# A tile of x that goes into its first product before its root is known

## The chip, the cores and the metric

The kernel runs on one core of a Trainium2 chip. Its metric is the time of one execution on the device in microseconds (us); three runs of the kernel before gave a median of 901.99 us (901.09 to 902.46). A profile comes from one more execution.

## The reference

One layer of an encoder in fp32 on x of 1024 tokens by 1024 channels:

```python
h = rmsnorm(x, norm_g[l])
proj = h @ w_in[l]
q, k, v, za, u, vs, zs, gm = jnp.split(proj, IN_SPLITS, axis=-1)
...
sgo = chunked_spatial_gating(jax.nn.gelu(u, approximate=False),
                             jax.nn.gelu(vs, approximate=False), ...)
...
x = x + y @ w_o[l]
return rmsnorm(x, final_g)

def rmsnorm(x, g):
    y = xf * lax.rsqrt(jnp.mean(xf * xf, axis=-1, keepdims=True) + EPS)
    return (y * g.astype(jnp.float32)).astype(x.dtype)
```

The change touches only the start: the first rmsnorm and the product of h with the columns for vs, which the kernel computes first. The root of a token multiplies its whole row of h, so it may be multiplied on after the product as well: (x * g) @ w times the root gives the same.

## The kernel before

**Products of split numbers.** An fp32 value is cast to fp32r (the high part), and the low part is the difference. A product is the sum of three fp32r matmuls of 128x512: high by high, high by low, low by high. All large products are made as blocks of two by two with seven block products instead of eight, from sums of blocks of h (the forms b11, t1, t2, b21, t3, b22, t4) and sums of blocks of the weights (a11, a12, s1 to s4, a22). `split` makes both parts: the cast on ACT (ScalarE), the difference on DVE (VectorE).

**The first stage.** x comes in eight tiles t of 128 tokens. `scale_of(t)` squares a tile on ACT with a row sum, and `rstd_of` makes the reciprocal root of it with a few small operations on DVE and one Sqrt on ACT. `turned_half` multiplies one half of the tile's channels by the root and by norm_g on DVE and transposes it in four 128x128 matmuls against `ident` into a PSUM bank of the tag sc, which has two banks. `form_of` splits the transposed half into a form. Tiles 0 to 3 (`first_tile`) give b11 and b21, tiles 4 to 7 (`second_tile`) t1 and b22, with raw sums that stay in `xh`. `first_product(t)` multiplies b11 of tile t by a11 (bank mm or tp) and b21 by a12 (bank o); ACT copies the second into `xh`, and `to_x11` adds the first later. Then `by_s1(t)` (t1 by s1, in banks o and sc), `by_s4(t)` (b22 by s4), and further the products of t2, t3 and t4.

**The head.** norm_g is spread over the partitions by matmuls of `ones_r` with its high and low halves (`spread`, into `g_in`); `keep_busy` issues matmuls whose results are not used, four ahead of the spreads and eight behind them.

**Order.** The tile framework orders the instructions of each engine when the program is built, and `after(second, first)` adds an order between two of them without a wait of its own. Each engine then works strictly in its order. The x tiles and weights come over SP's queue. The sums of weights are made by accumulating transfers that GpSimd issues (`add_on`, L606): two onto s1, two onto a11 (which becomes s2), two onto a12 (which becomes s4). ACT and DVE split s1 and s4 with `split_behind` (L651, L652). `feed` keeps the head's matmuls in the order in which they are written.

Lines that matter: L353 the products of later stages, L555 `keep_busy`, L573 `spread`, L619 the square, L629 the scaling, L634 the transposes, L647 and L648 the parts of a form, L674 and L675 the raw sum and the negative copy of `second_tile`, L683 `raw_t2`, L736 the low of the first weights, L750 the products of the first stage, L769 the copy out of bank o.

## Time and profile before

| | |
|---|---|
| median of three runs | 901.99 us |
| the profiled execution | 901.17 us, span 899.4 us |
| busy PE, DVE, ACT, POOL | 889.1, 685.8, 532.0, 149.8 us |
| mean granted TensorE clock | 0.998 |
| first matmul of a product starts | 9.79 us |
| PE idle: 0 to 10, 10 to 20, 880 to 899.4 us | 3.0, 0.5, 6.6 us |

PE is TensorE's matmuls, PEld its weight loads, POOL GpSimd. A row of the order of time has the start from the span's start, the time, engine, line, operation, tiles and count, and in brackets how long the engine was idle before it and what ended that. Times of a group of equal rows overlap at their ends: on ACT and DVE an operation starts about 0.1 us before the one ahead of it has ended, on PE 0.17.

### The profile page before, as it was taken

The page shows a single profiled execution, that of the slowest core. Times are in us where ns is not written, and L with a number is a line of the kernel's source. Part 1 is how long each engine was busy: PE and PEld are TensorE (multiplying, and loading weights), DVE is VectorE, ACT ScalarE, POOL GpSimd, SP SyncE. Part 2 cuts the span into 40 slices and gives each one's busy share as a digit, 9 for nine tenths or more (in the row PEclk, how much of TensorE's full clock was granted, in tenths as well). Part 3 has the DMA queues.
Part 4 walks back from the last instruction along what each step waited for, and adds up shares of the span by engine and source line. Part 5 has one row for each costly group of instructions (what it writes and reads, how often), then busy time and mean ns, then how long its engine had stood idle before and what let it go on. Part 6 is the DMA issues. An engine that isn't in the chain of part 4 may idle for free.

```text
span 899.4 us, 13233 instructions
## 1 busy us (share of the span) xinstructions
PE 889.1 (99%) x4304; PEld 743.7 (83%) x4304; DVE 685.8 (76%) x1251; ACT 532.0 (59%) x1064; POOL 149.8 (17%) x213
## 2 busy tenths in 40 slices
PE   8999999999999999999999999999999999999997
PEld 6788888888888888888888888888888888888885
DVE  7879966666687788888878888646796488479986
ACT  7875533334455567676777776755585376467453
POOL 2322222203030001111210111100121121110012
PEclk9999999999999999999999999999999999999999
DMA  9997888868778767878787788899899789998533
GB/s 327 215 258 218 263 208 175 165 157 260 259 253 284 214 188 213 216 151 214 178 221 227 248 241 194 232 316 365 308 284 376 288 226 259 301 301 282 186 116 118
DMA packets 132750, 213.77 MB, mean 238 GB/s; under 512 B 12777, under 2 KB 61161, under 8 KB 132682
## 3 DMA queue, kind: packets, MB, share of 16 engines
q1 hardware_dynamic: 110072, 149.74, 49.9%
q0 software_dynamic: 22464, 62.93, 31.4%
q8 instruction: 34, 0.56, 0.2%
q14 instruction: 34, 0.28, 0.1%
q10 hardware_dynamic: 146, 0.27, 0.1%
HBM read 147.74 MB, written 86.11 MB: 260 GB/s over the span
## 4 chain that ended last, share of the span: by engine, by line
PE 97%; DMA 1%; ACT 1%; DVE 0%; issue 0%; SPq 0%
PE ps_mm L353 42%; PE ps_o L353 27%; PE ps_tp L353 7%; PE ps_sc L1341 3%; PE ps_sc L353 3%; PE ps_tp L750 2%; PE ps_o L1428 2%; PE ps_tp L1387 2%; PE ps_mm L750 2%; PE ps_o L750 2%; PE ps_tp L1012 2%; PE ps_sc L750 1%; PE ps_sc L634 1%; DMA T_t3h<-in_w_dram 1%; ACT wh L162 0%
## 5 line engine op out<-in xcount | busy, mean ns | idle before, releaser
L162 ACT CAST wh<-s 128x1024 fp32r<-128x1024 f32 (+1 forms) x79 | 79.3, 1006 | 92.8 <-PE ps_mm L353 42.4
L163 DVE TENSOR_TENSOR wl<-wr,wh 128x512 fp32r<-128x512 f32 (+1 forms) x77 | 72.0, 936 | 53.2 <-ACT wh L162 52.6
L163 DVE TENSOR_TENSOR wl<-s,wh 128x1024 fp32r<-128x1024 f32 (+1 forms) x79 | 92.6, 1172 | 11.0 <-ACT wh L162 10.9
L162 ACT CAST wh<-wr 128x512 fp32r<-128x512 f32 (+1 forms) x77 | 63.1, 820 | 59.6 <-PE ps_mm L353 30.5
L353 PE MATMUL ps_o<-T_t1h,wh 128*128 128x512 f32 x148 | 58.6, 396 | 0.0
L353 PE MATMUL ps_o<-T_t1h,wl 128*128 128x512 f32 x148 | 57.7, 390 | 0.0
L353 PE MATMUL ps_o<-T_t1l,wh 128*128 128x512 f32 x148 | 57.6, 389 | 0.0
L1356 ACT ACTIVATE pr<-ps_sc,sm 128x192 f32<-128x192 f32 (+2 forms) x128 | 50.9, 410 | 7.4 <-DVE sm L1350 6.4
L353 PE MATMUL ps_mm<-T_t3h,wh 128*128 128x512 f32 x140 | 54.9, 392 | 0.0
L353 PE MATMUL ps_mm<-T_b11h,wh 128*128 128x512 f32 x140 | 54.9, 392 | 0.0
L353 PE MATMUL ps_mm<-T_b11l,wh 128*128 128x512 f32 x140 | 54.7, 391 | 0.0
L353 PE MATMUL ps_mm<-T_t3h,wl 128*128 128x512 f32 x140 | 54.7, 390 | 0.0
L353 PE MATMUL ps_mm<-T_b11h,wl 128*128 128x512 f32 x140 | 54.7, 390 | 0.0
L353 PE MATMUL ps_mm<-T_t2h,wl 128*128 128x512 f32 x140 | 54.6, 390 | 0.0
L353 PE MATMUL ps_mm<-T_t2h,wh 128*128 128x512 f32 x140 | 54.6, 390 | 0.0
L353 PE MATMUL ps_mm<-T_t2l,wh 128*128 128x512 f32 x140 | 54.5, 390 | 0.0
L353 PE MATMUL ps_mm<-T_t3l,wh 128*128 128x512 f32 x140 | 54.5, 389 | 0.0
L353 PE MATMUL ps_mm<-T_t4h,wh 128*128 128x512 f32 x136 | 53.6, 394 | 0.0
L353 PE MATMUL ps_mm<-T_t4h,wl 128*128 128x512 f32 x136 | 53.2, 391 | 0.0
L353 PE MATMUL ps_mm<-T_t4l,wh 128*128 128x512 f32 x136 | 52.9, 389 | 0.0
L307 POOL DMA_DIRECT2D sums<-in_w_dram x40 | 29.8, 939 | 91.6 <-ACT x L371 42.2
L353 PE MATMUL ps_o<-T_b22h,wh 128*128 128x512 f32 x108 | 42.7, 395 | 0.0
(420 smaller groups left out, 2448.2 us busy)
## 6 DMA issues: line engine op xcount, KB each, us to landing
wr<-in_w_dram SPq DMA_DIRECT2D x86, 256.0 KB
sums<-in_w_dram POOLq DMA_DIRECT2D x20, 512.0 KB, 7.0
s<-sums SPq DMA_DIRECT2D x20, 512.0 KB
q_hl<-qhl SPq DMA_DIRECT2D x16, 512.0 KB
q<-q_hl SPq DMA_DIRECT2D x64, 128.0 KB
y_dr<-x POOLq DMA_DIRECT2D x28, 256.0 KB, 6.7
g<-in_w_dram POOLq DMA_DIRECT2D x12, 512.0 KB, 6.6
wr<-in_w_dram SPq DMA_DIRECT2D x11, 512.0 KB
```

The source lines that it names most:

```text
L162: hi_of.append(nc.scalar.copy(hi, src))
L163: return nc.vector.tensor_sub(lo, src, hi.bitcast(F32))
L307: return lambda: paced(nc.gpsimd.dma_start(dst, src, accum_op=op))
L353: nc.tensor.matmul(acc, lt, rt, start=fresh and k == 0 and n == 0, stop=k == 3 and n == 2, skip_group_check=True,)
L634: turns.append(nc.tensor.transpose(pt[:, i * P : (i + 1) * P], xt[:, k * P : (k + 1) * P], ident[:]))
L750: mm = nc.tensor.matmul(acc[:], lt, rt, start=fresh and k == 0 and n == 0, stop=k == 3 and n == terms[-1], skip_group_check=True,)
L1012: nc.tensor.matmul(pm[:, t * P : (t + 1) * P], xh[:, half * 4 + t, g * P : (g + 1) * P], bias[-1][1][:, g % 4, :], start=True, stop=True,)
L1341: nc.tensor.matmul(sc[:, i, k0:], q_of[:, c, i * P : (i + 1) * P], kt[:, f, k0:], start=f == 0, stop=f == 1,)
L1356: nc.scalar.activation(held_in[c, i], sc[:, i, lo:hi], AF.Exp, bias=nmax[:, c, i : i + 1], scale=-1.0, accum_out=sums[:, c, i : i + 1],)
L1387: nc.tensor.transpose(dst, pr[:, i, block * P : block * P + width], ident[:])
L1428: nc.tensor.matmul(po[:, cs], lt, rt, start=n == 0, stop=n == len(terms) - 1)
```

## The change

Tile 0 no longer waits for its root. DVE multiplies it by norm_g alone (`turn_unscaled`), it is transposed, ACT copies it to `xh`, and eight plain fp32 matmuls (`unscaled_product`) take it as it is against the raw weights a11 and a12, unsplit. ACT multiplies the results in both banks by the root afterwards. For the later products tile 0's forms are made from the copies: `spread_root` lays the root along the columns (a diagonal on ACT, a matmul with ones, two copies on ACT), GpSimd multiplies both copies by it (`scale_unscaled`) and makes the low of b11, ACT and DVE make b21 (`split_unscaled`). The low parts of a form come last in tile 1's product, transposes of tiles 2 to 5 stand behind given matmuls of the products (`amid`), tile 5 is scaled ahead of the second low of s1, and tile 6 ahead of the lows of s4. The head has five matmuls of `keep_busy`, all ahead of the spreads; ones come from one memset, and the halves of norm_g are spread one after the other.

The build's order shows it. On ACT at the head, before, where wr_119 is tile 0, T_t3h and T_t3l the raw weights, ps_sc_196 and ps_sc_204 its turned halves:

```order
L619 ACTIVATE wT_154,st_21_159<-wr_119 128x1024
L137 ACTIVATE st_23_163<-st_21_159,eps_sb 128x1
L734 CAST wh_177<-T_t3h_171 128x512 x2
L162 CAST wh_211<-T_t3h_171 128x1024
L647 CAST T_b11h_150<-ps_sc_196 128x4x128
L619 ACTIVATE wT_154,st_31_183<-wr_175 128x1024
L647 CAST T_b21h_152<-ps_sc_204 128x4x128
```

And now, where ps_sc_168 and ps_sc_175 are the turned halves and st_27_163 is the finished root:

```order
L614 ACTIVATE wT_144,st_23_155<-wr_122 128x1024
L140 ACTIVATE st_25_159<-st_23_155,eps_sb 128x1
L696 ACTIVATE xh_119<-ident,st_27_163 128x128
L677 COPY xh_119<-ps_sc_168 128x512
L784 CAST wh_181<-T_t3h_149 128x512 x2
L677 COPY xh_119<-ps_sc_175 128x512
L165 CAST wh_192<-T_t3h_149 128x1024
```

The first half's copy now stands behind the diagonal, which reads the finished root.

On PE around tile 7, before (ps_o_581 is by_s4(1), wr_230 tile 7, ps_sc_663 by_s1(2)):

```order
L750 MATMUL ps_o_581<-wh_509,T_b22h_400 128x512
L634 MATMUL ps_sc_608<-ident,wr_230 128x128 x4
L750 MATMUL ps_o_581<-wh_509,T_b22h_400 128x512
L750 MATMUL ps_o_581<-wl_510,T_b22h_400 128x512 x2
L634 MATMUL ps_sc_618<-ident,wr_230 128x128 x4
L750 MATMUL ps_o_581<-wh_509,T_b22l_401 128x512 x2
L750 MATMUL ps_o_581<-wh_513,T_b22h_400 128x512 x2
L750 MATMUL ps_o_581<-wl_514,T_b22h_400 128x512 x2
```

And now (ps_o_563 is by_s4(1), wr_223 tile 7, ps_sc_645 by_s1(2)):

```order
L801 MATMUL ps_o_563<-wh_495,T_b22h_378 128x512 x2
L801 MATMUL ps_o_563<-wl_496,T_b22h_378 128x512 x2
L801 MATMUL ps_o_563<-wh_495,T_b22l_379 128x512 x2
L629 MATMUL ps_sc_590<-ident,wr_223 128x128 x4
L629 MATMUL ps_sc_600<-ident,wr_223 128x128 x4
L801 MATMUL ps_sc_645<-T_t2h_360,T_t1h_376 128x512 x2
```

Tile 7's transposes moved from the middle of by_s4(1) to its end, directly ahead of by_s1(2), whose bank has the tag of theirs.

On DVE around tile 6, now (wr_221 is tile 6, wl_492 and wl_496 the lows of s4, wr_223 tile 7); before, the two lows, L652, stood ahead of this scaling, with other rows between them:

```order
L624 SCALAR_TENSOR_TENSOR wr_221<-wr_221,st_107_539,xh_119 128x512 x2
L650 TENSOR_TENSOR wl_492<-T_t3l_150,wh_491 128x1024
L650 TENSOR_TENSOR wl_496<-T_t3l_150,wh_495 128x1024
L723 TENSOR_TENSOR xh_119<-xh_119,ps_sc_544 128x512
L643 TENSOR_TENSOR T_b22l_379<-ps_sc_554,T_b22h_378 128x4x128
L138 TENSOR_SCALAR st_112_579<-st_111_577 128x1
L643 TENSOR_TENSOR T_t1l_377<-xh_119,T_t1h_376 128x4x128
L142 RECIPROCAL st_114_583<-st_113_581 128x1
```

On ACT at the same place, before (st_113_599 is tile 7's root, ps_sc_572 tile 6's second half, ps_sc_618 tile 7's):

```order
L777 ACTIVATE xh_116<-ps_o_581 128x512
L137 ACTIVATE st_113_599<-st_111_595,eps_sb 128x1
L647 CAST T_b22h_400<-ps_sc_572 128x4x128
L675 ACTIVATE x_157<-ps_sc_562 128x512
L647 CAST T_t1h_398<-xh_116 128x4x128
L679 COPY T_t4l_402<-ps_sc_572 128x512
L647 CAST T_b22h_400<-ps_sc_618 128x4x128
L675 ACTIVATE x_158<-ps_sc_608 128x512
```

And now (st_113_581 is tile 7's root, ps_sc_590 and ps_sc_600 its halves):

```order
L642 CAST T_b22h_378<-ps_sc_554 128x4x128
L838 ACTIVATE xh_119<-ps_o_563 128x512
L724 ACTIVATE x_147<-ps_sc_544 128x512
L642 CAST T_t1h_376<-xh_119 128x4x128
L728 COPY T_t4l_380<-ps_sc_554 128x512
L140 ACTIVATE st_113_581<-st_111_577,eps_sb 128x1
L642 CAST T_b22h_378<-ps_sc_600 128x4x128
L724 ACTIVATE x_148<-ps_sc_590 128x512
```

Tile 7's root moved behind the copies and the second cast of tile 6; the cast of its second half ahead of the copy of its first is as it was.

The diff, cut to its core:

```diff
-    plain = mtile([P, D], F32, "wl", 3)[:, 0:HALF]
...
-    nc.vector.memset(plain, 1.0)
+    ones_r = mtile([P, 4, HALF], F32R, "T_b22l", 1)[:, 0, :]
+    g_both = mtile([P, 4, HALF], F32R, "T_t1h", 1)
+    nc.vector.memset(ones_r.bitcast(F32), 1.0)
...
+    for at, engine in ((0, nc.vector), (2, nc.gpsimd)):
+        engine.memset(g_both[:, at : at + 2, :].bitcast(F32), 0.0)
...
-    ones_r = slot("b22l", (P, HALF))
-    ones_made = nc.vector.tensor_copy(ones_r[:], plain)
...
-    keep_busy(4)
-    for n in range(2):
-        for half in range(2):
+    keep_busy(5)
+    for half in range(2):
+        for n in range(2):
             spread(n, half)
-    keep_busy(8)
...
-            after(square, casts[2 * t - 3])
+            after(square, casts[2 * t - 5])
...
-            if len(turns) == 1:
-                feed(turns[0])
+            if t == 1:
+                feed(turns[-1])
...
+    def first_half(t, j, xt, r):
+        name = ("b11", "b21")[j]
+        pt = turned_half(xt, r, j, t)
+        form_of(name, t, by_k(pt[:]))
+        if j:
+            return lambda: nc.scalar.mul(raw_b21(t), pt[:], -1.0)
+        return lambda: nc.scalar.copy(raw_sum(t), pt[:])
...
+    def unscaled(j):
+        return by_k((raw_sum, raw_b21)[j](0))
+    def turn_unscaled(j):
+        xg = x_place(0, 0, j)
+        nc.vector.tensor_mul(xg, x_in[0][:, half_of(j)], g_in[j][:])
+        pt = bank("sc")
+        for k in range(4):
+            feed(nc.tensor.transpose(pt[:, k * P : (k + 1) * P], xg[:, k * P : (k + 1) * P], ident[:]))
+        return nc.scalar.copy((raw_sum, raw_b21)[j](0), pt[:])
+    def unscaled_product(acc, j, *ks):
+        for k in ks:
+            feed(
+                nc.tensor.matmul(
+                    acc[:],
+                    unscaled(j)[:, k, :],
+                    raws[("a11", "a12")[j]][:, k, :],
+                    start=k == 0,
+                    stop=k == 3,
+                    skip_group_check=True,
+                )
+            )
+    def spread_root(r):
+        diagonal, *across = (x_place(1, 1, 0)[:, i * P : (i + 1) * P] for i in range(3))
+        nc.scalar.mul(diagonal, ident[:], r[:])
+        summed = bank("sc")[:, 0:P]
+        feed(nc.tensor.matmul(summed, ones_r[:, 0:P].bitcast(F32), diagonal, start=True, stop=True))
+        nc.scalar.copy(across[0], summed)
+        nc.scalar.mul(across[1], summed, -1.0)
+        return [v.unsqueeze(1).broadcast_to([P, 4, P]) for v in across]
+    def scale_unscaled(j, across):
+        return nc.gpsimd.tensor_mul(unscaled(j), unscaled(j), across[j])
+    def split_unscaled(j):
+        hi, lo = (v[:, :, tokens(0)] for v in hb[("b11", "b21")[j]])
+        raw = unscaled(j)
+        if j:
+            low = split(hi, lo, raw, True)
+            after(hi_of[-1], casts[5])
+            after(low, lows[5])
+            return
+        after(nc.scalar.copy(hi, raw), casts[3])
+        return nc.gpsimd.tensor_tensor(lo, raw, hi.bitcast(F32), op=ALU.subtract)
     def second_tile(t):
         xt, r = scale_of(t)
...
+                after(firsts[-1], turned[0])
                 first_lows.append(
                     (nc.gpsimd if k else nc.vector).tensor_tensor(
                         lo[:, ks], raw[:, k, :], hi[:, ks].bitcast(F32), op=ALU.subtract
...
         return mm
     accs = {}
+    steps = []
     t5s = {}
+    def amid(t, half, product, n):
+        turn, step = turns[8 * (t - 1) + 4 * half], steps[24 * (product - 1) + n]
+        after(turn, step)
     def first_product(t):
         accs[t] = bank("mm" if t < 2 else "tp")
-        terms = (0, 1, 2) if t else (0, 2, 1)
-        vs_product(accs[t], "b11", t, "a11", True, terms=terms)
         m2 = bank("o")
-        vs_product(m2, "b21", t, "a12", True, terms=terms)
+        for acc, name, weight in ((accs[t], "b11", "a11"), (m2, "b21", "a12")):
+            if t == 1:
+                vs_product(acc, name, t, weight, True, terms=(0, 1))
+                vs_product(acc, name, t, weight, False, terms=(2,))
+            else:
+                vs_product(acc, name, t, weight, True)
         nc.scalar.copy(x_place(0, 0, t), m2[:])
     def to_x11(t):
...
     def keep_t5(t):
         nc.scalar.copy(x_place(0, 1, t), t5s[t][:])
-    first = scale_of(0)
     for name, at in (("a11", "t3h"), ("a12", "t3l")):
         raws[name] = slot(at, dt=F32)
     load_vs(0)
     load_vs(1)
     x_in[1] = load_x(1)
-    first_lows = []
+    first_lows, firsts = [], []
+    _, root = scale_of(0)
+    turned = [turn_unscaled(j) for j in range(2)]
+    after(turned[0], of_root[0])
...
+    unscaled_product(accs[0], 0, 0, 1)
+    unscaled_product(accs[0], 0, 2, 3)
+    split_vs(1)
+    after(hi_of[0], turned[1])
     second = scale_of(1)
-    unsplit = first_tile(0, first)
-    after(of_mean[1], lows[0])
-    after(first_lows[0], scalings[1])
-    after(lows[0], first_lows[0])
-    split_vs(1)
-    after(first_lows[2], lows[0])
-    after(lows[1], first_lows[2])
-    after(casts[0], hi_of[0])
-    after(squares[1], casts[0])
-    after(casts[1], squares[1])
+    after(squares[1], hi_of[0])
+    after(of_mean[1], first_lows[2])
     for c in (2, 3):
         load_vs(c)
     x_in[2] = load_x(2)
...
-    for c in (2, 3):
-        split_vs(c)
-        after(first_lows[c + 1], lows[1])
-        after(hi_of[c - 1], casts[1])
-    for move in unsplit:
+    m2 = bank("o")
+    split_vs(2)
+    after(hi_of[1], of_root[1])
+    unscaled_product(m2, 1, 0, 1)
+    across = spread_root(root)
+    unscaled_product(m2, 1, 2)
+    split_vs(3)
+    left = [first_half(1, 0, *second)]
+    unscaled_product(m2, 1, 3)
+    left.append(first_half(1, 1, *second))
+    after(hi_of[2], hi_of[1])
+    after(first_lows[3], scalings[1])
+    after(first_lows[4], first_lows[3])
+    after(lows[0], first_lows[4])
+    copied = left.pop(0)()
+    m2_kept = nc.scalar.mul(x_place(0, 0, 0), m2[:], root[:])
+    after(m2_kept, copied)
+    for move in left:
...
-    for c in range(2):
-        add_on(flat(two_k(raws["s1"], c)), w_vs(1, 1, c))
-    for c in range(2):
-        add_on(flat(two_k(raws["a11"], c)), flat(two_k(raws["s1"], c)))
-    for c in range(2):
-        add_on(flat(two_k(raws["a12"], c)), flat(two_k(raws["a11"], c)))
+    sums_begun = [add_on(flat(two_k(raws["s1"], c)), w_vs(1, 1, c)) for c in range(2)]
+    sums_begun += [add_on(flat(two_k(raws["a11"], c)), flat(two_k(raws["s1"], c))) for c in range(2)]
+    sums_begun += [add_on(flat(two_k(raws["a12"], c)), flat(two_k(raws["a11"], c))) for c in range(2)]
...
-    first_tile(1, second)
-    after(scalings[2], first_lows[4])
+    first_tile(2)
+    after(of_mean[2], lows[0])
+    after(lows[1], scalings[3])
+    after(squares[2], casts[0])
+    after(casts[1], of_root[2])
+    after(m2_kept, casts[1])
+    after(nc.scalar.mul(accs[0][:], accs[0][:], root[:]), casts[3])
...
-    first_tile(2)
-    first_product(0)
...
+    after(of_mean[3], lows[1])
+    after(lows[3], scalings[4])
...
+    amid(2, 0, 1, 13)
+    amid(2, 1, 1, 18)
+    for j in range(2):
+        after(scale_unscaled(j, across), sums_begun[1])
+    after(sums_begun[2], split_unscaled(0))
+    after(sums_begun[3], sums_begun[2])
+    after(sums_begun[4], sums_begun[3])
...
-        split_behind(hi, lo, two_k(raws["s1"], c))
+        low_of_s1 = split_behind(hi, lo, two_k(raws["s1"], c))
...
-    second_tile(4)
+        if c == 0:
+            second_tile(4)
...
+    amid(3, 0, 2, 7)
+    amid(3, 1, 2, 13)
+    split_unscaled(1)
...
-    for c in range(2):
-        split_w("s4", c, behind=True)
+    amid(4, 0, 3, 3)
+    amid(4, 1, 3, 9)
+    amid(5, 0, 3, 17)
+    amid(5, 1, 3, 21)
+    after(low_of_s1, scalings[9])
+    lows_of_s4 = [split_w("s4", c, behind=True) for c in range(2)]
...
+    after(lows_of_s4[0], scalings[11])
+    after(highs_behind[2], of_root[6])
```

More of the change, by code (lines that the diff above doesn't have):

```diff
@@ L554, in keep_busy @@
         for _ in range(n):
-            feed(nc.tensor.matmul(idle[:], ones_r[:, 0:P], ones_r[:], start=True, stop=True))
+            feed(nc.tensor.matmul(idle[:], ones_r[:, 0:P], ones_r, start=True, stop=True))
     idle = bank("sc")
     g_in = [bank("tp") for half in range(2)]
-    g_both = slot("t1h")
     g_parts = [g_both[:, 2 * n : 2 * n + 2, :] for n in range(2)]
-    for half in range(2):
-        after(nc.vector.memset(g_parts[0][:, half, :].bitcast(F32), 0.0), ones_made)
-    nc.gpsimd.memset(g_parts[1].bitcast(F32), 0.0)
     for half in range(2):
@@ L574, in spread @@
         )
-    keep_busy(4)
-    for n in range(2):
-        for half in range(2):
+    keep_busy(5)
+    for half in range(2):
+        for n in range(2):
             spread(n, half)
-    keep_busy(8)
     hb = new_b(("b11", "b21"))
@@ L648, in form_of @@
             lows.append(nc.vector.tensor_sub(lo, src, hi.bitcast(F32)))
+    highs_behind = []
     def split_behind(hi, lo, src):
[L651 to L666 removed]
+        highs_behind.append(nc.scalar.copy(hi, src))
+        after(highs_behind[-1], casts[-1])
+        low = nc.vector.tensor_sub(lo, src, hi.bitcast(F32))
+        after(low, lows[-1])
+        return low
@@ L717, in split_w @@
         hi, lo = pair_of_w()
-        (split_behind if behind else split)(hi[:], lo[:], flat(two_k(raws[name], c)) if src is None else src)
+        low = (split_behind if behind else split)(hi[:], lo[:], flat(two_k(raws[name], c)) if src is None else src)
         keep_w(name, c, hi, lo)
+        return low
     def split_vs(c):
@@ L733, in split_vs @@
                 ks = half_of(k)
[L734 removed]
+                firsts.append(nc.scalar.copy(hi[:, ks], raw[:, k, :]))
+                after(firsts[-1], turned[0])
                 first_lows.append(
```

25 lines of the change are left out of this document (8 added, 17 removed).

## The prediction

> **What bounds the kernel now.** I read the page's first part, then the stretches of time, then the first 52 us of PE, ACT and DVE in order of time.
>
> ```profile
> span 899.4 us, 13233 instructions
> PE 889.1 (99%) x4304; PEld 743.7 (83%) x4304; DVE 685.8 (76%) x1251; ACT 532.0 (59%) x1064; POOL 149.8 (17%) x213
> ```
>
> TensorE is busy in 889.1 of 899.4 us, so an edit pays only by ending PE's idle time or its work. The stretches say where the idle 10.3 us are (columns: stretch, length, then busy time and count of PE, PEld, DVE, ACT, POOL, then granted clock, DMA share, GB/s).
>
> ```profile
> 0.00:10.00 10.00, 7.00 (x25) 4.90 (x26) 6.70 (x15) 7.00 (x12) 2.99 (x9) 1.00 0.80 284
> 10.00:20.00 10.00, 9.46 (x43) 7.02 (x43) 8.97 (x20) 8.89 (x17) 1.92 (x2) 1.00 1.03 388
> 40.00:50.00 10.00, 9.92 (x51) 7.72 (x50) 9.31 (x22) 6.30 (x14) 4.04 (x5) 1.00 1.00 243
> 60.00:80.00 20.00, 20.00 (x90) 16.56 (x89) 15.69 (x24) 16.37 (x22) 4.25 (x6) 1.00 0.79 237
> 160.00:880.00 720.00, 720.00 (x3498) 605.22 (x3497) 545.61 (x987) 433.18 (x901) 102.93 (x148) 1.00 0.82 242
> 880.00:899.40 19.40, 12.78 (x68) 10.89 (x66) 12.63 (x36) 6.45 (x18) 5.05 (x6) 0.93 0.28 108
> ```
>
> 3.0 us lie in the first ten, 0.5 in the second, 6.6 in the last 19.4. From 60 to 80 and from 160 to 880 PE is busy without a break, so what the change delays or gains before 60 us arrives at the end one for one. And from 40 to 50 DVE is busy 9.31 of 10 us: there PE runs only just ahead of it.
>
> **Up to the first product.** The head on PE, then ACT and DVE (start, length, instruction, idle time before and what ended it):
>
> ```profile
> 2.19 2.08 PE L555 MATMUL ps_sc<-T_b22l 128*128 128x512 f32 x4 [2.19 <-DVE T_b22l L544]
> 4.07 1.81 PE L573 MATMUL ps_tp<-T_t1h,T_b22l 128*128 128x512 f32 x4
> 5.71 2.02 PE L555 MATMUL ps_sc<-T_b22l 128*128 128x512 f32 x8
> 9.79 0.73 PE L750 MATMUL ps_mm<-wh,T_b11h 128*128 128x512 f32 x2 [0.71 <-ACT T_b11h L647]
> ...
> 4.50 1.06 ACT L619 ACTIVATE wT<-wr 128x1024 f32<-128x1024 f32 x1 [0.27 <-DMA wr<-in_x_dram]
> 5.68 0.29 ACT L137 ACTIVATE st<-st,eps_sb 128x1 f32<-128x1 f32 x1
> 13.24 0.59 ACT L663 COPY xh<-ps_sc 128x512 f32<-128x512 f32 x1
> ...
> 3.81 1.28 DVE L568 TENSOR_TENSOR T_t1h<-wh,T_t1h 1x512 fp32r<-1x512 f32 x2 [0.59 <-ACT T_t1h L567]
> 6.01 0.16 DVE L139 RECIPROCAL st<-st 128x1 f32<-128x1 f32 x1 [0.17 <-ACT st L137]
> 6.91 1.41 DVE L629 SCALAR_TENSOR_TENSOR wr<-wr,st,ps_tp 128x512 f32<-128x512 f32 x2
> ```
>
> Before, the first useful product starts at 9.79; the 12 fillers of L555 are no useful work. Now: the cast L544, which ended PE's first wait, goes, so fillers start about a 512-column DVE operation (0.7) before 2.19, near 1.5, five of them ahead of the four spreads. The spreads still wait for the halves of norm_g (L568, 3.81 to 5.09); both of the first half come first now, so g_in[0] is there near 5.1 and g_in[1] near 5.9. The new multiplications by norm_g cost half of L629's row each, 0.66 start to start: they end near 5.9 and 6.8. Between and behind them stand the small operations of the root. From the reciprocal at 6.01 to the scaling at 6.91 they took 0.9; behind the second multiplication that ends near 7.6 (6.81 before). On ACT the diagonal (L696) needs the finished root and stands ahead of the copy of the turned half 0, as the order in the part on the change shows. ACT thus idles from 5.97 to 7.65 with that copy queued behind, though its transposes are done by 6.6. The diagonal, 128x128, lies between the 0.29 of the one-column root and the 0.59 of a 512-column copy, nearer the first: 0.3. The copy takes 0.59. The first plain product can start at 7.65 + 0.3 + 0.59 = 8.5: 1.3 earlier.
>
> **The plain products.** Matmul pairs in steady state, the wait before tile 1, its transposes, and a group of four transposes later on:
>
> ```profile
> 12.94 0.62 PE L750 MATMUL ps_o<-wh,T_b21h 128*128 128x512 f32 x2
> 13.39 0.62 PE L750 MATMUL ps_o<-wh,T_b21l 128*128 128x512 f32 x2
> ...
> 16.23 1.17 PE L634 MATMUL ps_sc<-ident,wr 128*128 128x128 f32 x8 [0.41 <-DVE wr L629]
> 17.53 0.73 PE L750 MATMUL ps_mm<-wh,T_b11h 128*128 128x512 f32 x2
> ...
> 20.43 0.63 PE L634 MATMUL ps_sc<-ident,wr 128*128 128x128 f32 x4
> 20.81 0.48 PE L750 MATMUL ps_o<-wh,T_b21h 128*128 128x512 f32 x1
> ```
>
> A fp32r matmul of 512 columns costs 0.455 / 2 = 0.227. From 9.79 to 17.53 (7.74) PE did tile 0's 24 (5.45), spent 1.3 on transposes (16.23 to 17.53) and waited the remaining 1.0, 0.41 of it for tile 1's scaling. The 24 become eight plain fp32 matmuls, of which the trace has none. Lower end: one such row, 0.227 each, 1.8 in all. Upper end: a full product of two numbers split in high and low is four products; the kernel spends three, so 4 x 0.227 = 0.91 each and 7.3 in all. I take the upper end: the kernel's own three products leave one out and are the nearest row to a full-width result. With 0.25 for the root's spread, and 1.1 for eight transposes (8 x 0.11 and the refill), tile 1's product starts at 8.5 + 7.3 + 0.25 + 1.1 = 17.15, 0.4 earlier. At the lower end tile 1's own chain sets it (square, root, scalings and transposes, behind the same ACT casts): near 15.4, 2.1 earlier.
>
> The Trainium skill, "FP8 and Floating Point Precision", section "TensorE Precision Notes", gives true FP32 four passes through the array; by it the sum would be the upper end's. No run shown so far bears on it.
>
> **Tiles 1 to 5.** The matmuls are the same in number. From tile 1's product to tile 5's first transposes PE has 66 matmuls (15.0) and six groups of four transposes; a group moves the next matmul by 0.38 plus some 0.1 (row 20.43 to 20.81), 2.8 in all. So the half-0 transposes of tile 5 stand at 17.15 + 17.8 = 35.0, against 36.03 before for both halves. This is the last place with a gain.
>
> **Tiles 6 and 7.** The rows of before:
>
> ```profile
> 36.03 1.18 PE L634 MATMUL ps_sc<-ident,wr 128*128 128x128 f32 x8
> 41.74 1.23 DVE L652 TENSOR_TENSOR wl<-T_t3l,wh 128x1024 fp32r<-128x1024 f32 x1 [0.30 <-ACT wh L651]
> 42.88 0.16 DVE L139 RECIPROCAL st<-st 128x1 f32<-128x1 f32 x1
> 43.72 1.42 DVE L629 SCALAR_TENSOR_TENSOR wr<-wr,st,xh 128x512 f32<-128x512 f32 x2
> 45.23 0.69 DVE L674 TENSOR_TENSOR xh<-xh,ps_sc 128x512 f32<-128x512 f32 x1
> 45.84 0.16 DVE L139 RECIPROCAL st<-st 128x1 f32<-128x1 f32 x1
> 47.17 0.74 DVE L629 SCALAR_TENSOR_TENSOR wr<-wr,st,xh 128x512 f32<-128x512 f32 x1
> ...
> 44.57 0.29 ACT L137 ACTIVATE st<-st,eps_sb 128x1 f32<-128x1 f32 x1
> 46.42 0.61 ACT L675 ACTIVATE x<-ps_sc 128x512 f32<-128x512 f32 x1
> 49.98 0.59 ACT L647 CAST T_b22h<-ps_sc 128x512 fp32r<-128x512 f32 x1 [1.96 <-PE ps_sc L634]
> 50.47 0.60 ACT L675 ACTIVATE x<-ps_sc 128x512 f32<-128x512 f32 x1
> 51.62 0.61 PE L750 MATMUL ps_sc<-T_t2h,T_t1h 128*128 128x512 f32 x2
> ```
>
> Before, tile 7's two groups of transposes lay inside by_s4(1), and by_s1(2) followed at 51.62 without a wait; its bank had come free when ACT's L675 (50.47 + 0.60) had read tile 7's first half. Now all matmuls of by_s4 stand ahead of tile 7's transposes and by_s1(2) directly behind them (order of PE in the part on the change). It needs that same bank, and on ACT the cast of the second half stands ahead of the copy of the first. From the last transpose PE must therefore wait for its end (0.2), the cast (49.98 to 50.47: 0.49) and the copy (0.60), about 1.3. Nothing covers it: PE has no other instruction in between.
>
> When do these transposes come? By DVE's order: from 35.7 the sub of tile 5 (0.60, as 45.23 to 45.84), scaling of its second half (0.66), low of s1 (1.23 by row 41.74, 1.14 start to start), two form lows (1.2), two sums of raw_t2 with a short wait for ACT (1.6), to 40.8; small operations to the scaling (42.88 to 43.72: 0.84), tile 6's scaling (1.33), both weight lows (2.3), sub of tile 6 (0.60): 45.9. ACT then does three copies at 0.49 and only then tile 7's root (0.3), 47.7; before, that root came at 44.57, ahead of them. From the reciprocal to the scaling 1.33 (45.84 to 47.17): 49.1, against 47.17. First half scaled at 49.9, second at 50.6; transposes 50.0 and 50.7 to 51.1, with PE waiting 0.5 and 0.2; with the wait of 1.3 by_s1(2) starts at 52.4 to 52.6. That is 0.8 to 1.0 later than 51.62.
>
> SP's queue keeps its rows and order; the loads of x that wait until tiles 0 to 2 are turned are read several tiles later. Tile 0's forms cost PE nothing: GpSimd's multiplications and its low lie behind the two sums onto s1, and DVE loses one low.
>
> ```profile
> 7.26 1.28 POOL L736 TENSOR_TENSOR wl<-T_t3h,wh 128x512 fp32r<-128x512 f32 x1 [4.97 <-ACT wh L734]
> 24.60 0.86 POOL L606 DMA_DIRECT2D T_t3h<-T_t4h  x1 [7.58 <-DVE T_t1l L629]
> 35.03 0.85 POOL L606 DMA_DIRECT2D T_t3l<-T_t3h  x1 [1.70 <-DVE st L150]
> 40.63 1.08 ACT L651 CAST wh<-T_t3l 128x1024 fp32r<-128x1024 f32 x1
> ```
>
> Three operations of 1.28 (row 7.26) end near 26.2, behind ACT's cast near 24.9; the third sum, issued at 24.60 before, is then issued 1.6 later. The sixth, issued at 35.03, was read by the cast at 40.63; that cast moves to 41.2. Cover 0.5 plus whatever it had landed early; gone, each us late is a us at by_s4. Taken as nothing.
>
> **Sum.** At the first product -1.3; PE's own work after it 8.65 instead of 7.74, +0.9; so -0.4 at tile 1. Then the start of by_s1(2) by its chain, 52.5 against 51.62: +0.9. The same by PE's waits: -0.4, plus 2.0 at tile 7 (0.5, 0.2, 1.3), less the 0.08 that PE idled there from 40 to 50 before: +1.5, if no small wait on the way goes. I take +1.0, nearer the chain, which follows single rows. It is carried to the end. The profiled execution took 901.17 (span 899.4), so 902.2; the median of the three runs is 0.82 above it, 901.99, so 903.0.
>
> **The rivals.** (1) Slower: the clock. Fillers and spreads ran 0.427 apart from 2.19 to 5.35, and 0.23 from 5.71 on (2.08 and 2.02 for 4 and 8): half speed and full, though the granted clock's column shows 1.00 for the whole stretch, so the spacing is the witness. PE had then been busy 3.5 us without a break. The eight fillers behind the spreads are gone; from 5.9 to 8.5 PE has eight transposes and idles half the time. Granted by 5, as busy from 1.5 suggests, nothing happens. If it isn't granted by 8.5, a plain product costs 4 x 0.427 = 1.71, 0.8 more each; one or two are hit before the clock comes: 903.8 to 904.6. It decides once the grant comes after 8.5. The Trainium skill, "TensorE: Matmul & The Clock Gate", Parts 1 and 4, says the activity window is free-running and transposes do not count as busy; that rule speaks against this change. This trace, with full speed 3.5 us after the first matmul, cannot tell a free-running window from one that starts with the work. (2) The GpSimd sums land late: by_s4 waits 0.5 to 1.5 more: 903.5 to 904.5. For it: the third is issued 1.6 later; against: the casts that read the last two come later too. (3) Plain products are cheap: PE is at tile 1 by 15.4, but the waits at tile 7 stay since orders are fixed and DVE is full: about -0.1, 901.9. (4) Faster: cheap products and a DVE that keeps pace, so that 2.1 comes through less the 1.3 or less: 899.9 to 901.2. Little speaks for it: DVE's 9.31 of 10 us.
>
> **How the numbers follow.** Forecast 0.50 (903.0, own range 902.0 to 903.8); clock 0.22; late sums 0.12; cheap products 0.10; faster 0.06. About 0.2%, 1.8 us, is what a measurement of this kernel tells from no change: 900.2 to 903.8. The clock's case is slower but for its lowest end (0.20), late sums in half (0.06), the forecast's upper edge with unknown waits 0.10: slower 0.36. Faster: 0.05 of the last case. Same: 0.59. The range 901.2 to 905.0 leaves out the faster case and, above, two hits of the clock together with late sums.
>
> **What would show it.** Right: the first plain product near 8.5 behind ACT's copy, 0.9 per plain product, tile 1's product near 17.1, an idle time of 1.3 on PE ahead of by_s1(2) at 52.5, ended by ACT's copy of tile 7. Wrong: rows at half clock behind 8.5; by_s4 waiting for a weight low; no idle time at 52.

## The result

The changed kernel takes 904.96 us (median of 16 runs, 902.05 to 907.26) against 901.31 us of the kernel before (16 runs, 900.62 to 902.46). The ratio is 1.0039, 95% interval 1.0029 to 1.0049: slower by some 3.5 us, twice what a measurement of this kernel can tell from no change. It lies inside the range that was given (901.2 to 905.0), but at its upper edge. The likeliest forecast, 903.0 and no change that can be measured, was wrong: "slower" had the smaller chance, 0.36. The runs also spread over 5.2 us, those of before over 1.8.

The profiled execution took 902.81 us and is one of the quickest of the 16. Its page, and its stretches (columns as before):

```profile
span 901.0 us, 13209 instructions
PE 889.2 (99%) x4291; PEld 741.2 (82%) x4291; DVE 684.8 (76%) x1248; ACT 532.6 (59%) x1068; POOL 153.2 (17%) x216
```

```profile
0.00:10.00 10.00, 7.18 (x21) 4.05 (x22) 5.32 (x12) 6.59 (x13) 2.15 (x9) 1.00 0.80 300
10.00:20.00 10.00, 9.87 (x37) 5.73 (x35) 8.78 (x18) 9.00 (x17) 5.31 (x5) 1.00 1.03 373
40.00:50.00 10.00, 9.68 (x48) 7.70 (x47) 9.25 (x20) 6.29 (x12) 5.89 (x7) 1.00 1.00 262
160.00:880.00 720.00, 719.48 (x3493) 604.29 (x3493) 544.45 (x985) 431.27 (x897) 102.65 (x148) 1.00 0.82 242
```

PE's idle time up to 20 us fell (7.18 and 9.87 busy against 7.00 and 9.46). From 40 to 50 it grew (9.68 against 9.92), and from 160 to 880, where PE had not paused at all, 0.5 us is idle. The rows of PE at the places of the prediction:

```profile
1.45 2.50 PE L555 MATMUL ps_sc<-T_b22l 128*128 128x512 f32 x5 [1.45 <-DVE T_b22l L103]
8.41 3.70 PE L683 MATMUL ps_mm<-T_t3h,xh 128*128 128x512 f32 x8 [1.02 <-ACT xh L677]
11.95 1.88 PE L683 MATMUL ps_o<-T_t3l,xh 128*128 128x512 f32 x4
16.40 0.71 PE L801 MATMUL ps_mm<-wh,T_b11h 128*128 128x512 f32 x2
20.21 0.63 PE L629 MATMUL ps_sc<-ident,wr 128*128 128x128 f32 x4 [0.35 <-DVE wr L624]
34.87 0.60 PE L629 MATMUL ps_sc<-ident,wr 128*128 128x128 f32 x4
49.72 1.18 PE L629 MATMUL ps_sc<-ident,wr 128*128 128x128 f32 x8 [0.32 <-DVE wr L624]
52.08 0.74 PE L801 MATMUL ps_sc<-T_t2h,T_t1h 128*128 128x512 f32 x2 [1.18 <-ACT x L724]
...
758.39 0.50 PE L356 MATMUL ps_mm<-T_t4h,wh 128*128 128x512 f32 x1 [0.40 <-DVE x L429]
```

The first plain product starts at 8.41, tile 1's product at 16.40 (17.53 before), tile 5's half-0 transposes at 34.87 (36.03 before). At tile 7 the gain is gone: PE waits 0.32 for DVE's scaling and 1.18 for ACT's copy, and by_s1(2) starts at 52.08 (51.62 before). Two things are not in the prediction: the wait of 0.35 ahead of tile 2's transposes, and the wait at 758.39. In this trace by_s1(2) is 0.46 late and the end 1.6. So the trace shows less than half of the 3.5 us. The rest had to be looked for in other executions of the same kernel.

### The profile page after: what moved, and what is told of

It is laid out like the page before. It is cut to its first block, busy times and chain, and to the rows that moved or that the text cites. A ratio compares the mean times of both kernels' runs of the same rounds, so it can differ in the third digit from the quotient of the medians.

```text
span 901.0 us, 13209 instructions
## 1 busy us (share of the span) xinstructions
PE 889.2 (99%) x4291; PEld 741.2 (82%) x4291; DVE 684.8 (76%) x1248; ACT 532.6 (59%) x1068; POOL 153.2 (17%) x216
## 4 chain that ended last, share of the span: by engine, by line
PE 95%; DVE 3%; ACT 1%; issue 0%; DVEq 0%; ACTq 0%
PE ps_mm L356 42%; PE ps_o L356 27%; PE ps_tp L356 6%; PE ps_sc L1434 3%; PE ps_sc L356 3%; PE ps_tp L801 2%; PE ps_o L1521 2%; PE ps_tp L1480 2%; PE ps_mm L801 2%; PE ps_tp L1105 2%; PE ps_sc L801 1%; PE ps_o L801 1%; PE ps_sc L629 0%; DVE wr L624 0%; PE ps_sc L555 0%
## 5 line engine op out<-in xcount | busy, mean ns | idle before, releaser
L166 DVE TENSOR_TENSOR wl<-wr,wh 128x512 fp32r<-128x512 f32 (+1 forms) x77 | 71.9, 935 | 52.8 <-ACT wh L165 52.1
L166 DVE TENSOR_TENSOR wl<-s,wh 128x1024 fp32r<-128x1024 f32 (+1 forms) x79 | 92.2, 1167 | 11.5 <-ACT wh L165 11.3
```

Source lines behind the costliest of these rows:

```text
L166: return nc.vector.tensor_sub(lo, src, hi.bitcast(F32))
```

## The experiments

The theories at the start: the wait at tile 7 makes the loss (the prediction's step); the software sums land late (its second rival); the clock (its first rival). A fourth came out of the first traces: GpSimd's multiplications stop DVE. A fifth came out of the traces of the repaired kernels: the change shifts the places where PE's code is fetched. Medians of the kernels that were timed, each against runs of the kernel before on the same chip:

| kernel | median us | ratio to before | 95% interval |
|---|---|---|---|
| changed kernel | 904.96 | 1.0039 | 1.0029 to 1.0049 |
| sums_first | 905.27 | 1.0046 | 1.0033 to 1.0059 |
| clock_kept | 904.45 | 1.0034 | 1.0021 to 1.0046 |
| late_forms | 902.59 | 1.0014 | 1.0005 to 1.0023 |
| root7 | 902.29 | 1.0009 | 1.0000 to 1.0018 |
| two | 901.01 | 0.9995 | 0.9985 to 1.0004 |
| three | 900.52 | 0.9991 | 0.9982 to 1.0000 |
| pad10 | 900.21 | 0.9987 | 0.9979 to 0.9996 |
| pad20 | 901.96 | 1.0009 | 1.0000 to 1.0017 |
| best | 899.72 | 0.9981 | 0.9972 to 0.9990 |

**The changed kernel again.** No edit; two more executions with a trace.

> The changed kernel itself, unaltered, one more execution with its trace; the runs of it lie between 902 and 907, and the first trace was of one of the quickest (span 901.0). If the time is lost where the prediction put it (tile 7), this trace too has idle times of about 0.3 and 1.2 ahead of tile 7's transposes and of by_s1(2), and whatever it takes beyond 902.8 lies elsewhere. If the software sums land late, the sixth sum (landed at 40.1 in the first trace) lands later by as much as the run is longer, the casts of s4 (39.9) and the scaling of tile 6 (41.3) follow it, and PE waits ahead of by_s4 or at tile 7. If the clock is late, the first plain products are 1.7 apart instead of 0.86.

> As the look before: a third execution of the changed kernel. Tile 7's wait: idle times of 0.3 and 1.2 at 49.7 and 52.1. Late sums: the sixth sum lands behind 40.1 and by_s4 or tile 7 waits longer. Late clock: plain products 1.7 apart behind 8.4. If the time beyond 902.8 lies in none of these, PE's idle time after 60 shows it.

They took 904.63 and 903.76. Tile 7's two waits are the same in both (0.34 and 1.18), but by_s1(2) starts at 53.08 and 53.09, a whole us later than in the first trace: something ahead of tile 7 varies. In look1 it is the clock. PE's first product, then stretches of look1:

```profile
8.26 5.40 PE L683 MATMUL ps_mm<-T_t3h,xh 128*128 128x512 f32 x8 [1.02 <-ACT xh L677]
```

```profile
6.00:8.00 2.00, 1.08 (x8) 0.60 (x6) 1.13 (x5) 0.74 (x3) 0.00 (x0) 1.00 1.02 410
9.00:10.00 1.00, 1.00 (x2) 0.34 (x1) 0.45 (x1) 1.00 (x3) 0.68 (x1) 0.50 1.05 430
10.00:11.00 1.00, 1.00 (x3) 0.39 (x2) 0.29 (x1) 1.00 (x2) 0.59 (x1) 0.50 1.02 418
```

The granted clock (third column from the end) is 0.50 at 9 to 11, and the four plain products of the first bank took 5.40 instead of 3.70. The trace's clock records put full speed from 4.91 to 8.32, half from 8.32 to 11.73, full from then on: the clock had been granted and was taken back, after a window in which PE idled almost half the time. In look2 the clock stayed and another row is long. DVE's root of tile 2, GpSimd's multiplications, and PE's wait:

```profile
17.76 2.03 DVE L145 SCALAR_TENSOR_TENSOR st<-st,st 128x1 f32<-128x1 f32 x1
```

```profile
16.92 2.85 POOL L704 TENSOR_TENSOR xh<-xh 128x512 f32<-128x512 f32 x2
```

```profile
21.22 0.63 PE L629 MATMUL ps_sc<-ident,wr 128*128 128x128 f32 x4 [1.17 <-DVE wr L624]
```

An operation on one column that takes 0.22 elsewhere took 2.03. It ends at 19.79, GpSimd's second multiplication at 19.77. In the first trace it was the next such operation, less long:

```profile
18.13 1.04 DVE L153 TENSOR_TENSOR st<-st,st 128x1 f32<-128x1 f32 x1
```

```profile
16.24 2.92 POOL L704 TENSOR_TENSOR xh<-xh 128x512 f32<-128x512 f32 x2
```

It ends at 19.17, GpSimd's work at 19.16. This is where PE's 0.35 ahead of tile 2 comes from. A row shortly ahead of it was stopped too, by the first multiplication alone, which by the trace ended at 17.90:

```profile
17.57 0.34 DVE L145 SCALAR_TENSOR_TENSOR st<-st,st 128x1 f32<-128x1 f32 x1
```

**Tile 7's root and scaling early** (root7):

```diff
-    highs_behind = []
+    highs_behind, negated = [], []
...
-        nc.scalar.mul(nf12[t - 4][:], pt[:], -1.0)
+        negated.append(nc.scalar.mul(nf12[t - 4][:], pt[:], -1.0))
...
     after(second_tile(7), move)
+    after(negated[2], of_root[7])
+    after(lows[10], scalings[12])
+    after(lows[11], scalings[12])
```

> The changed kernel with one thing more: ACT takes tile 7's root ahead of the negated copy of tile 6's first half, and DVE scales tile 7's first half ahead of tile 6's two form lows. If tile 7's wait is the loss, PE has no idle time at 49 to 52 any more (0.32 and 1.18 go), by_s1(2) starts near 50.3, and the median falls by 1.5 to 1.9 from the changed kernel's, to about 903.2. If the sums landing late (or anything else that varies) makes the loss, the median falls by less than 0.7 and the spread of the runs stays at 5.

Measured 902.29: 2.7 below the changed kernel, more than the 1.5 to 1.9 expected. Tile 7's transposes lie inside by_s4(1) again and by_s1(2) follows without a wait (51.93, not the 50.3 expected), although this trace had the longest stop of DVE of all:

```profile
15.29 4.26 DVE L166 TENSOR_TENSOR s<-T_t3l,s 128x1024 fp32r<-128x1024 f32 x1
```

```profile
15.64 2.83 POOL L704 TENSOR_TENSOR xh<-xh 128x512 f32<-128x512 f32 x2
```

```profile
20.21 1.19 PE L801 MATMUL ps_mm<-wh,T_b11l 128*128 128x512 f32 x4 [1.97 <-DVE st L138]
```

DVE's low of 1024 columns, 1.22 elsewhere, took 4.26: GpSimd's work ends at 18.47, and 1.08 later, most of its own time, so does the low. The wait at tile 7 is thus a true part of the loss, but not all of it.

**The third sum early** (sums_first), by orders on GpSimd alone:

```diff
-        after(scale_unscaled(j, across), sums_begun[1])
-    after(sums_begun[2], split_unscaled(0))
+        scaled = scale_unscaled(j, across)
+        after(scaled, sums_begun[1])
+        after(sums_begun[2], scaled)
     after(sums_begun[3], sums_begun[2])
-    after(sums_begun[4], sums_begun[3])
+    low_of_b11 = split_unscaled(0)
+    after(low_of_b11, sums_begun[3])
+    for later in sums_begun[4:]:
+        after(later, low_of_b11)
```

> The changed kernel with GpSimd's low of tile 0 (1.29) issued behind the third and fourth software sums instead of ahead of them, so that the third is issued when the first has landed (near 23.6 instead of 26.2). If late sums make the loss: the third sum lands near 30, the sixth near 38 instead of 40.1, the median falls by 1 to 3 and the spread of the runs from 5 to about 2. If tile 7's wait is the loss: the time stays within 0.3 of the changed kernel's, since DVE's order holds tile 6's scaling at 41.3 whatever the sums do.

Measured 905.27, the changed kernel within the error. GpSimd's issues of the third and fifth sum, here and then in the changed kernel:

```profile
24.30 0.87 POOL L601 DMA_DIRECT2D T_t3h<-T_t4h  x1 [4.92 <-DVE st L153]
...
32.58 0.86 POOL L601 DMA_DIRECT2D T_t3l<-T_t3h  x1 [2.66 <-DMA T_t3h<-T_t4h]
```

```profile
26.20 0.87 POOL L601 DMA_DIRECT2D T_t3h<-T_t4h  x1
...
32.78 0.85 POOL L601 DMA_DIRECT2D T_t3l<-T_t3h  x1 [4.10 <-DVE st L138]
```

The third sum was issued 1.9 earlier, but the fifth, which needs it landed, only 0.2 earlier: an earlier issue hardly moved the landings. So this kernel alone does not decide. ACT's casts that read the last two sums do, here in the changed kernel's first trace:

```profile
39.90 1.99 ACT L648 CAST wh<-T_t3l 128x1024 fp32r<-128x1024 f32 x2
```

They start without a wait in every trace. The sixth sum landed at 40.13 in this one (39.92 before the change) and was read by the second cast at 40.84. Late sums are not the loss, and this rival falls.

**More fillers** (clock_kept):

```diff
         for n in range(2):
             spread(n, half)
+    keep_busy(3)
```

> The changed kernel with three more fillers behind the spreads of norm_g (some 0.7 of work ahead of the transposes of x times norm_g, in time in which PE idles, since the copy on ACT is not due before 7.65). In two of the four traces so far of kernels with the change's head (look1, sums_first) the granted clock went back to 0.50 from 8.3 to 11.7, and eight records of plain products took 5.40 instead of 3.70. Clock theory: with the fillers no trace shows 0.50 between 5 and 890, the eight records take 3.70, and the median falls by 0.5 to 1.0 (about half of the executions times 1.0 to 1.7), with no change at tile 7. Port theory: waits for DVE of 0.35 to 2 near 20 remain, and where the clock stays the times are those of look2 and of the first trace, 902.8 to 904: the median falls by less than 0.5.

Measured 904.45. Its trace kept the clock (3.70 for the eight records) and had DVE's stop (2.35 instead of 0.22, PE waits 1.50). The step from 1.0039 to 1.0034 lies inside the intervals, so what the clock costs the median is not shown.

**GpSimd's multiplications later** (late_forms). All orders stay; GpSimd alone waits until DVE has scaled tile 2:

```diff
-        after(scale_unscaled(j, across), sums_begun[1])
+        scaled = scale_unscaled(j, across)
+        after(scaled, sums_begun[1])
+        behind(scaled, scalings[3])
```

> The changed kernel, its orders unchanged, but GpSimd's two multiplications of tile 0's forms wait until DVE has scaled tile 2 (scalings[3]), so that they run from about 19.8 to 22.7 instead of 16 to 19.5. Port theory: DVE operations with two operands in SBUF stood still until GpSimd's two multiplications had ended (1.04 instead of 0.16, 2.03 instead of 0.22, in root7 4.26 instead of 1.22); here none of DVE's operations from 14 to 20 is longer than usual, PE's idle time ahead of tile 2's transposes (0.35, 1.17, in root7 1.97) goes, and the median falls by 0.5 to 1.5. Clock theory alone: no change of the median beyond 0.3, and 5.40 in part of the traces. If GpSimd has nothing to do with it, DVE's long operations come back at another place.

Measured 902.59, 2.4 below the changed kernel, more than the 0.5 to 1.5 expected. The same DVE rows as above, and GpSimd's:

```profile
15.36 1.22 DVE L166 TENSOR_TENSOR s<-T_t3l,s 128x1024 fp32r<-128x1024 f32 x1
...
17.41 0.22 DVE L145 SCALAR_TENSOR_TENSOR st<-st,st 128x1 f32<-128x1 f32 x1
...
17.86 0.16 DVE L153 TENSOR_TENSOR st<-st,st 128x1 f32<-128x1 f32 x1
...
21.67 0.49 DVE L145 SCALAR_TENSOR_TENSOR st<-st,st 128x1 f32<-128x1 f32 x1
```

```profile
19.61 2.53 POOL L704 TENSOR_TENSOR xh<-xh 128x512 f32<-128x512 f32 x2 [3.66 <-DVE wr L624]
```

All three have their usual length. What moved is the next root, tile 3's, stretched from 0.22 to 0.49 until GpSimd ended at 22.14, where DVE has time to spare. One wait on GpSimd, which is no bottleneck, brought back two thirds of the loss: the stops of DVE by GpSimd are shown. Tile 7's waits are still there in this trace (0.33 and 1.18), so this gain is not root7's.

**Both, and with the fillers** (two = root7 and late_forms; three = two and clock_kept).

> Three without its three fillers: tile 7 early and GpSimd's multiplications behind tile 2's scaling. If the clock takes a share, part of the executions run the first plain products at half speed, the spread is wider than three's (899.7 to 902.1) and the median lies 0.3 to 0.8 above 900.5. If the fillers do nothing, the median is 900.5 within 0.2. Port and tile 7 theory: 4.0 to 4.5 below the changed kernel's 904.96.

> All three repairs on the changed kernel: tile 7's root and scaling early (as root7), GpSimd's multiplications behind tile 2's scaling (as late_forms), three fillers (as clock_kept). If these three causes are the whole loss, tile 1's product starts near 16.3, by_s1(2) near 50.2 without a wait (51.6 before), and the median is 1 to 1.5 below that of the kernel before, some 4.5 below the changed kernel's. If something behind 60 us loses more (the traces of the changed kernel lose another 0.8 to 1.9 from 230 to 760), it lies 0.2 to 0.5 below before or level with it.

Two measured 901.01, three 900.52. Alone the two repairs bring 2.7 and 2.4, together 4.0: they overlap. That what DVE loses at 18 us is handed down DVE's order to tile 7's scaling is the likely reason and was not tested. The 0.5 of the fillers lies inside the intervals again. Three's trace is 2.09 ahead of before's at 54 us, yet only 0.55 at the end. Something behind 60 us gives the gain back.

**The kernel before again.** No edit.

> The kernel before, unaltered, a second execution with its trace. All traces of the changed kernel fall behind the first trace of before by 0.2 to 1.3 at 230 to 320 and by 0.4 to 0.7 at 757. If this belongs to the change, this trace lies within 0.2 of the first one from 60 on; if it varies from execution to execution, it shows steps of its own at these places.

It took 901.50. It runs 0.22 behind the first trace of before at 54 us (its clock was granted at 8.24, not 5.62, and its first product starts at 10.04, not 9.79) and 0.32 at the end, with one step of 0.32 near 320 and none at 757. So the step at 757 belongs to the change.

**PE's code at its old places** (pad10, pad20: ten or twenty small matmuls on top of three, behind its three fillers; best: ten, still smaller, where PE waits for ACT's first copy).

```diff
     keep_busy(3)
+    for _ in range(10):
+        feed(nc.tensor.matmul(idle[:, 0:64], ones_r[:, 0:P], ones_r[:, 0:64], start=True, stop=True))
```

> The kernel of three with ten small matmuls more (128x64 into the fillers' bank, behind the three fillers, in PE's idle time), so that PE's stream of instructions has as many matmuls and weight loads as before the change and its code is fetched at the same instructions as before. Three's trace was 2.09 ahead of before at 54 us and only 0.55 ahead at the end: 1.2 lost from 303 to 312, 0.67 at 757, where a software sum that ACT casts at 740 landed 9.2 after its issue (8.0 in both traces of before) and a 16 KB fetch of code ran within it (at 730.1 to 731.9, issue 730.6; before: 730.1 to 731.1, issue 731.8). Code theory: the sum takes 8.0 again, the step at 757 goes, and the median falls by 0.5 to 1.2, to about 899.6. Transfer theory (the transfers themselves are the bound at these places, so that PE cannot keep a lead of over some 1 us): steps of the same size stay and the median stays at 900.5.

> As pad10 with twenty small matmuls: ten more than before the change. PE's code is then fetched about 1 us of PE's work earlier than before. Code theory: it matters where the fetches fall, and the steps at 303 to 312 and 757 change in size (gone or larger), with the sum at 740 between 8.0 and 9.2. Transfer theory: the steps are those of three. Either way some 0.3 is lost at the first product, since the transposes come later.

The wait at 757 goes back to ACT, which waits at 740 for a software sum (bq). By that ACT is late for a low on DVE, and DVE, which does not pause again, is late to read out the bank that PE takes at 757. These are DVE's rows now, and its reading of that bank before:

```profile
743.96 1.23 DVE L166 TENSOR_TENSOR wl<-s,wh 128x1024 fp32r<-128x1024 f32 x1 [0.68 <-ACT wh L165]
...
757.66 0.67 DVE L429 TENSOR_TENSOR x<-x,ps_mm 128x512 f32<-128x512 f32 x1
```

```profile
756.01 0.68 DVE L426 TENSOR_TENSOR x<-x,ps_mm 128x512 f32<-128x512 f32 x1
```

GpSimd's issue of this sum, then ACT's cast, before the change, with the transfers between the two (queue, packets, MB, share):

```profile
731.84 0.86 POOL L205 DMA_DIRECT2D bq<-bq  x1 [1.10 <-DVE wl L163]
```

```profile
739.88 1.06 ACT L157 ACTIVATE T_t2h<-bq 128x1024 fp32r<-128x1024 f32 x1 [0.46 <-DMA bq<-bq]
```

```profile
q0 software_dynamic: 306, 1.12, 75.8%
q1 hardware_dynamic: 295, 0.81, 26.8%
```

And in the changed kernel:

```profile
732.71 0.86 POOL L208 DMA_DIRECT2D bq<-bq  x1 [1.11 <-DVE wl L166]
```

```profile
741.93 1.06 ACT L160 ACTIVATE T_t2h<-bq 128x1024 fp32r<-128x1024 f32 x1 [1.64 <-DMA bq<-bq]
```

```profile
q0 software_dynamic: 358, 1.27, 72.8%
q1 hardware_dynamic: 427, 1.04, 30.7%
q8 instruction: 1, 0.02, 0.6%
```

8.04 from issue to cast before, 9.22 now. Between them lies one packet of q8 that is not there in before: 16 KB of code, which took 0.95 by the trace. q8 has 34 such packets in a whole run, about one for every 252 of PE's 4291 matmuls and as many weight loads, and this one starts at PE's 3569th to 3578th matmul record in all fourteen traces: it is taken to be PE's own code. The change takes 13 matmul records out of the head, so the fetch falls 6 to 10 matmuls, or some 1.4 to 2.3 us, later in the work that both kernels share (733.2 here, 730.1 before, where 0.9 is PE's lag). In all nine traces with 4291 or 4294 records this sum took 8.9 to 9.35 and a fetch ran in it, wholly or in part; in all five with 4304 or more (two of before, pad10, pad20, best) it took 8.0 to 8.2 and the fetch had ended. That the fetch holds up the sum's packets on an engine that both use is the likely mechanism and was not measured. Pad10 measured 900.21 (899.6 was expected), with no step at 757, though its small matmuls delay the first product to 8.90 (three: 8.23). Pad20 measured 901.96: no step at 757 either, but its trace, with the clock granted only at 7.43, starts the first product at 10.85.

> The kernel of three, with the ten small matmuls (128x16 here) behind tile 0's transposes instead of ahead of them, where PE waits for ACT's copy until 8.2 anyway: PE's code is fetched at the same instructions as before, and the first plain product is not delayed (pad10: 8.90, three: 8.23). Code theory: the sum at 740 takes 8.0 to 8.1 from its issue, there is no step at 757, the trace is 1.9 to 2.2 ahead of before at 54 us, and the median lies at 899.4 to 900.0, 0.2 to 0.8 below pad10's 900.21. If pad10's gain over three (0.3) was chance, the median stays at 900.5 and the step of 0.67 at 757 comes back.

Best measured 899.72, ratio 0.9981 (0.9972 to 0.9990): faster than before by 1.7 (by the ratio) and than the changed kernel by 5.2. Its trace, PE and then ACT:

```profile
8.48 3.68 PE L685 MATMUL ps_mm<-T_t3h,xh 128*128 128x512 f32 x8
...
49.31 0.63 PE L631 MATMUL ps_sc<-ident,wr 128*128 128x128 f32 x4
49.69 0.71 PE L803 MATMUL ps_sc<-T_t2h,T_t1h 128*128 128x512 f32 x2
```

```profile
737.96 1.06 ACT L160 ACTIVATE T_t2h<-bq 128x1024 fp32r<-128x1024 f32 x1 [0.61 <-DMA bq<-bq]
```

No wait at tile 7, by_s1(2) at 49.69, the sum in 8.19, and a lead of 1.81 at 54 us that is 2.07 at the end: nothing was given back. Against three it differs in ten small matmuls alone. The losses between 100 and 320 us (0.4 to 2.2 in the other traces with the changed head, 0.2 in the second of before, none in best) were not traced to a cause: pad10, with PE's code at its old places, lost 0.6 there too. They stay open, and they are not small: in the three traces of the changed kernel they are 0.4, 1.6 and 0.7, beside 0.6, 1.6 and 1.6 lost by 54 us and 0.7, 0.4 and 0.4 at 757.

## Why the prediction was right or wrong

**The head, right.** First plain product: 8.5 said, 8.41 measured (8.18 to 8.60 in the other traces without pad10's and pad20's small matmuls), behind ACT's copy, which stood behind the diagonal as read from the order.

**The plain products, right.** 0.91 each was taken, at the upper end. Eight records from 8.41 to 11.95 are four matmuls: 0.885 each. What the Trainium skill's "FP8 and Floating Point Precision", section "TensorE Precision Notes", says of true FP32 (four passes) agrees with that time: it is 3.9 times 0.227, though the profile shows two records for each matmul, not four. Cheap products, the third rival, fell. Tile 1's product was said for 17.15 and came at 16.40: the transposes and the root's spread were sized 0.4 too long together, and the plain products 0.2.

**Tile 7, right in kind.** 1.3 was said for the bank behind ACT's copy, 1.18 measured; 0.5 for the scaling, 0.32 measured. The said time of by_s1(2), 52.4 to 52.6, lies between 52.08 of the first trace and 53.1 of the others. Root7 shows the wait as a cause. Why its removal brought 2.7, not 1.5, is not shown; the order that makes the wait may also pass DVE's stops on to PE.

**GpSimd's forms, wrong: the step that failed.** "Tile 0's forms cost PE nothing: GpSimd's multiplications and its low lie behind the two sums onto s1, and DVE loses one low." They lie there on GpSimd, but in four of the six traces in which they run at that place they stop DVE for 1.0 to 3.0, in the stretch in which PE waits for DVE. The prediction priced GpSimd's work on GpSimd and on its sums, and never asked what DVE does while it runs. Taken at zero, it was worth 2.4 (late_forms). The Trainium skill had it: "SBUF — State Buffer", section "Who interferes with whom", says that a DVE instruction with two SBUF inputs contends with a GpSimd instruction that reads SBUF, and that the ports they share are an exclusive lock. The traces agree: the operations that stopped (L145, L153, L166) read two tiles in SBUF; those with a PSUM input, or one input, kept their length between them.

**"From 60 to 80 and from 160 to 880 PE is busy without a break, so what the change delays or gains before 60 us arrives at the end one for one", wrong.** A PE without idle time has no slack, but the other engines have little more: at 757 before, the bank came free 0.2 ahead of its use. Taking 10 or 13 records out of PE's instructions moved a fetch into a sum, and 0.4 to 0.7 was lost there in all nine such traces.

**The clock, right as a rival, wrong as a mechanism.** The prediction had it granted late or not at all, and said that nothing happens if it is granted by 5. In two of the seven traces of kernels with the changed head and no added fillers (look1, sums_first) it was granted at 4.9 and taken back at 8.3, which made the first product 1.7 longer. In these two, DVE waits for ACT while GpSimd multiplies, and hardly stops (by 0.1 in sums_first, not at all in look1): the two losses take each other's place, which may be why a repair of the clock alone moved the median little.

**Late sums, wrong as a rival.** The sixth sum landed 0.2 later than before the change, and the cast that reads it came 0.7 after that.

**The range, right in part by luck.** Tile 7's wait was forecast. GpSimd's stops (2.4 alone), the fetch at 757 and the losses between 100 and 320 us were no terms of it; its upper end, 905.0, was meant for the clock and for late sums.

## What to carry to other kernels

Work that is put on GpSimd "beside the rest" has to be priced on DVE too: look at what DVE runs in that stretch, and whether its operations read two tiles in SBUF. Fillers that are cut out of PE's head may have been what kept the clock, and the number of instructions taken out moves every later fetch of code; where the kernel is tuned to a few tenths, compare several executions before and after, at a mark behind the edit and at the end. If the difference at the end is not the one at the mark, part of it does not lie where the edit is.

## What the runs showed of the hardware that had not been expected

- In three traces DVE stopped until GpSimd had ended both of its multiplications, not the first: 2.03, 2.35 and 4.26 for operations of 0.22, 0.22 and 1.22. In the first trace it got its turn between them: the first multiplication released the operation of 0.34, the second the one of 1.04. What decides this is not shown.
- An operation on a single column stops as a wide one does (1.04 and 2.03 instead of 0.16 and 0.22).
- The first matmul started at 1.45 or 1.46 in every trace with the changed head, and the clock records put full speed between 4.91 and 7.43, so between 3.46 and 5.98 later; full and half speed in look1 lasted 3.41 each. The Trainium skill, "TensorE: Matmul & The Clock Gate", Part 1, calls the window free-running and 3413 ns long; these traces agree. In the window behind the grant PE was recorded busy 1.87 and 1.91 of 3.41 where the clock went; where it stayed, 2.13 to 2.50 in six traces and 3.16 to 3.41 in the other four with the changed head, and 3.32 and 3.17 in the two of before. By these figures the first trace kept its clock by 0.2. The longest pause in the window does not decide: 1.02 where the clock went, and 1.02 in root7, where it stayed.
- One 16 KB fetch of code within a software sum went with 0.8 to 1.3 more from its issue to its use than the 8.04 of before. The Trainium skill, "Runtime: NRT & Kernel Launch", section "Instruction fetch mechanics", gives blocks of 16 KiB for 256 instructions, which agrees with one packet for about 252, and calls their cost mostly hidden; hidden it was for PE, not for the transfer that it met.
